# Two more gate tiles as a block-product pair, and a projection summed in two parts

## The chip, the core and the metric

The kernel runs on one core of one Trainium2 chip, as one program with one launch. The metric is the device time of the program in microseconds, the median of several runs. TensorE (PE) does the matmuls, VectorE (DVE) and ScalarE (ACT) the elementwise work, GpSimd (POOL) a little of it, and DMA queues, most of them issued from SyncE (SP), move data between HBM and on-chip memory. Each engine takes its own instructions in the order in which the built program lists them and waits on semaphores for the others.

## The reference

One layer of a two-branch backbone runs on 640 tokens (128 prompt and 512 sample tokens) of width 1024. The part that matters here:

```python
h = x * (1.0 + scale1) + shift1
proj = h @ p['w_in']
q, f_fwd, f_bwd, i_raw, g_raw, hy, mg = jnp.split(proj, SPLIT_IDX, axis=-1)
o_a, s_f, s_b = hgrn2_mixer(q, f_fwd, f_bwd, i_raw, g_raw, lb, ...)     # 8 heads, a scan
o_b = hyena_mixer(hy, p, row_len)                                       # a long convolution
gate_a, gate_b = jnp.split(jax.nn.sigmoid(mg), 2, axis=-1)
mix = (gate_a * (o_a @ p['proj_a']) + gate_b * (o_b @ p['proj_b'])) @ p['w_out']
x = layer_norm(ALPHA * x + gate1 * mix, p['ln1_g'], p['ln1_b'])
```

Inside `hgrn2_mixer` each head's output is divided by its root mean square before `o_a` is projected. A SwiGLU block with a second norm follows. All is float32; the outputs are the tokens of both groups and the final scan states.

## The kernel before

**Tiles and precision.** A dense product for one tile of 128 output channels is done in two halves of 320 tokens. Each float32 operand is split into a rounded high part (a cast, on ACT or DVE) and a low part (a subtraction, mostly on DVE), and three products of the parts are added: 8 slices of the inner dimension times 3 passes are 24 matmuls of 128x320 for a half, 48 for a tile (`dense_fm`). Its weights (512 KB) are loaded into a buffer `raw` by SP and split into `wh` and `wl`, three buffers of each (`issue`, `advance`; `LOOK` says by weight how many are prepared ahead).

**Stages.** The work runs in this order: filters and the modulation vectors; the *product stage* (tiles named m...); the long convolution (hy, fw, inv, then pb, its projection); the *scan stage* of the first branch (f, g, kT, sc, u, o, msp, mga, pa); `w_out` and the first norm (wo); SwiGLU (fa, fb, fc, fo) and the second norm.

**The product stage.** Pairs of tiles of `w_in` are not done densely: with two tiles and two halves of tokens the output is a 2x2 block product, for which class `Wino` needs 7 products of 12 matmuls instead of 8 of them, with sums of weights and of operands ahead and sums of results behind. `M1_ORDER` lists the pairs, and `PLAN` the order of steps: `g13` loads the first weight row of pair 13 and `w13` the second one and makes the sums and splits; `613` is product 6 of pair 13. Products 1, 6, 7, 4 of a pair add up in one bank of PSUM (`ma`): after 6 and after 7 ACT copies the bank (`mu`) before the next product adds to it. Products 5 and 3 share bank `mc`, and product 2 has `mb`. A finished tile goes to a DRAM tensor (`sd`) and is loaded again in its stage (`spilled`). There are 14 pairs; of the gate `mga` (`gate_a`, 8 tiles) tiles 4 to 7 come this way, tiles 0 to 3 are dense in the scan stage.

**The scan stage.** `HGSEQ` lists its steps: `a7 b7 q7 g7` make or load the inputs of head 7, `e7` (`hg_elem`) is its long elementwise chain on DVE and ACT, `s7` (`hg_scan`, `hg_post`) its matmuls: transposes kT of a tile t6, scores sc, states u, outputs o, and the mean square msp. Tiles t4 to t7 have one buffer, so the chain of a head writes them after the scan of the head before has read them. `c` (`comb_open`) opens the memory of the projection and splits heads 0 to 5 (`oah`, `oal`), `m0` to `m7` provide the gate tiles (`gate_unit`), `t` (`hg_tail`) norms and splits heads 6 and 7, `p0` to `p7` (`proja_unit`) project, multiply by the gate and add the other branch's part.

**What sets the order.** A scheduler places each engine's instructions when the program is built, by the order of the steps and its own estimate of when things are ready; an instruction may be placed ahead of others that were written earlier. `order_after` forces one behind another. Matmuls of dense gate tiles are placed where the scan's own matmuls would leave gaps.

## Time and profile before

| | |
|---|---|
| median of 3 runs | 1414.06 us (1412.3 to 1414.61) |
| the profiled execution | 1413.15 us, its span 1411.4 us |
| PE busy | 1371.7 us of the span |
| DVE, ACT, POOL busy | 995.7, 620.0, 63.4 us |
| product stage, from its first ma to the first matmul of the convolution (hy) | 115.5 us to 309.8 us |
| dense gate tiles, start of the first and the last mga matmul | 813.7 us and 858.7 us |

All times below are of this one profiled execution, counted from the start of its span. In a timeline a row gives start, duration, engine, line, operation and tiles (out<-in), and in brackets how long the engine stood idle before it and what it had waited for. Matmuls overlap: each shows some 0.31 us at 128x320, but starts 0.147 us after the one before, so costs are counted from start to start. A row of the waits gives who waited for whom, the total in us, how many times, and the longest.

### The profile page before, as it was taken

What the parts mean: (1) busy time and instruction counts of PE and PEld (TensorE: products, weight loads), DVE (VectorE), ACT (ScalarE), POOL (GpSimd) and SP (SyncE); (2) the same over time, 40 slices, a digit from 0 to 9 for tenths busy, and PEclk for the clock granted to TensorE, in tenths of its full rate; (3) what the DMA queues carried; (4) which work ended last, traced back from release to release, by engine and by line L of the source; (5) the groups of instructions that cost most, each with busy time, mean ns of one, the idle gap of its engine ahead of it and who ended that gap; (6) DMA issues with size and microseconds to landing.
All of it is one profiled execution on the core that took longest, in us unless ns stands there. A gap on an engine that the chain in (4) does not pass through costs nothing. (4 is left out here: it accounts for less than half of the span.)

```text
span 1411.4 us, 23424 instructions
## 1 busy us (share of the span) xinstructions
PE 1371.7 (97%) x9513; PEld 1290.8 (91%) x9513; DVE 995.7 (71%) x1752; ACT 620.0 (44%) x1010; POOL 63.4 (4%) x56
## 2 busy tenths in 40 slices
PE   4999999999999999999999999999999999999997
PEld 2689889899999999999999999988999999998886
DVE  6886786656889743648888786568987776765426
ACT  3555554442323211536655655227654443542121
POOL 4230000010000000000000000000000000000003
PEclk9999999999999999999999999999999999999999
DMA  7944666675323373432222223551653213267211
GB/s 246 334 139 146 208 207 195 184 232 193 101 83 102 90 246 131 135 115 82 81 86 77 64 63 109 174 196 75 169 162 102 81 59 118 89 201 263 75 60 75
DMA packets 198855, 195.63 MB, mean 139 GB/s; under 512 B 7581, under 2 KB 155773, under 8 KB 197980
## 3 DMA queue, kind: packets, MB, share of 16 engines
q1 hardware_dynamic: 194860, 179.75, 40.5%
q0 software_dynamic: 2160, 9.15, 1.8%
q10 hardware_dynamic: 1728, 5.24, 0.9%
q8 instruction: 74, 1.21, 0.4%
q14 instruction: 33, 0.27, 0.1%
HBM read 162.91 MB, written 31.21 MB: 138 GB/s over the span
## 5 line engine op out<-in xcount | busy, mean ns | idle before, releaser
L182 DVE TENSOR_TENSOR wl<-raw,wh 128x1024 fp32r<-128x1024 f32 x96 | 117.3, 1223 | 133.1 <-ACT wh L358 132.3
L358 ACT CAST wh<-raw 128x1024 fp32r<-128x1024 f32 x90 | 94.1, 1049 | 220.9 <-PE pb L612 41.0
L1431 PE MATMUL fo<-wh,act 128*128 128x512 f32 (+1 forms) x440 | 130.7, 380 | 0.0
L1431 PEld LDWEIGHTS fo<-wh,act 128*128 128x128 f32 x440 | 81.2, 188 | 16.0
L1431 PE MATMUL fo<-wl,act 128*128 128x512 f32 (+1 forms) x220 | 83.4, 379 | 0.0
L612 PE MATMUL hy<-hTh,wh 128*128 128x320 f32 x256 | 79.6, 311 | 0.0
L612 PE MATMUL hy<-hTh,wl 128*128 128x320 f32 x256 | 79.1, 309 | 0.0
L612 PE MATMUL hy<-hTl,wh 128*128 128x320 f32 x256 | 79.1, 309 | 0.0
L612 PE MATMUL f<-hTh,wh 128*128 128x320 f32 x224 | 70.7, 316 | 0.0
L612 PE MATMUL f<-hTl,wh 128*128 128x320 f32 x224 | 69.7, 311 | 0.0
L612 PE MATMUL f<-hTh,wl 128*128 128x320 f32 x224 | 69.2, 309 | 0.0
L182 POOL TENSOR_TENSOR y<-y,gb 128x512 f32<-128x512 f32 x8 | 11.6, 1454 | 888.4 <-ACT y L171 888.1
L1431 PEld LDWEIGHTS fo<-wl,act 128*128 128x128 f32 x220 | 41.3, 188 | 7.9
L612 PEld LDWEIGHTS hy<-hTh,wh 128*128 128x128 f32 x256 | 48.1, 188 | 0.0
L612 PEld LDWEIGHTS hy<-hTl,wh 128*128 128x128 f32 x256 | 48.1, 188 | 0.0
L612 PEld LDWEIGHTS hy<-hTh,wl 128*128 128x128 f32 x256 | 48.0, 188 | 0.0
L171 ACT ACT_TABLE_LOAD x36 | 46.2, 1283 | 1.4 <-PEq L1791 0.7
L715 PE MATMUL v<-wl,hTh 128*128 128x256 f32 x160 | 45.0, 286 | 1.6 <-DVE wl L182 1.6
L715 PE MATMUL v<-wh,hTl 128*128 128x256 f32 x160 | 45.1, 284 | 0.1
L715 PE MATMUL v<-wh,hTh 128*128 128x256 f32 x160 | 44.9, 285 | 0.0
L612 PEld LDWEIGHTS f<-hTl,wh 128*128 128x128 f32 x224 | 42.2, 188 | 0.0
L612 PEld LDWEIGHTS f<-hTh,wh 128*128 128x128 f32 x224 | 42.1, 188 | 0.0
(2293 smaller groups left out, 4699.6 us busy)
## 6 DMA issues: line engine op xcount, KB each, us to landing
raw<-in_w_in SPq DMA_DIRECT2D x52, 512.0 KB, 3.8
araw<-in_ada_w SPq DMA_DIRECT2D x20, 1024.0 KB, 6.5
rm<-in_w_in SPq DMA_DIRECT2D x28, 512.0 KB, 4.6
rp<-in_ffn_w_in SPq DMA_DIRECT2D x24, 512.0 KB, 5.4
raw<-in_ffn_w_out SPq DMA_DIRECT2D x22, 512.0 KB, 4.6
rf<-in_ffn_w_in SPq DMA_DIRECT2D x18, 512.0 KB, 5.2
sd<-my SPq DMA_DIRECT2D x28, 320.0 KB, 2.3
kk<-kd SPq DMA_DIRECT2D x20, 256.0 KB, 2.7
```

The source lines that it names most:

```text
L171: r = S.activation(out, in_, func, bias=bias, scale=scale)
L182: return (eng or V).tensor_tensor(out=out, in0=a, in1=b, op=op)
L358: (V.tensor_copy if HIE[i] == "V" else S.copy)(hi, raw)
L612: r = PE.matmul(ps[:, 0:HT], w[a][:, k, :], x[b][:, k, c0:c0 + HT], start=k == 0 and i == 0, stop=k == kt - 1 and i == 2)
L715: PE.matmul(ps[:, (t - t0) * 256:(t - t0) * 256 + 256], hT[b][:, k, t * P:t * P + P], w[a][:, k % 4, :], start=k == 0 and i == 0, stop=k = ...
L1431: PE.matmul(ps, x(t, b, k0 + kk), w[a][:, kk, :], start=first and kk == 0 and i == 0, stop=last and kk == nk - 1 and i == 2)
```

## The change

Gate tiles 2 and 3 of `mga` become pair 14 of the product stage and are then loaded like tiles 4 to 7. Tile 1's matmuls are ordered behind the last o matmul of head 7. Projection tiles 0 and 1 are done in two steps each: `r0 r1` sum over heads 0 to 5 in four banks that stay open, `z0 z1` add heads 6 and 7 and finish. Three entries of `LOOK` (weights 58 to 60) go from 2 to 1.

```diff
 M1_ORDER = (
...
-('mga', 6, 7))
+('mga', 6, 7), ('mga', 2, 3))
...
-                dense_fm(w[0], hT, half, ps)
+                dense_fm(w[0], hT, half, ps, after=hg.get(("end", H - 1)) if j and tag == "mga" else None)
...
-                PE.matmul(o, st[:, 1, 4 - b], q128[:, 1, cs], start=False, stop=True)
+                hg["end", h] = PE.matmul(o, st[:, 1, 4 - b], q128[:, 1, cs], start=False, stop=True)
...
+        elif op == "r":
+            U(proja_first(h), w_fm(I["proj_a"][0], h * P))
+        elif op == "z":
+            U(proja_unit(h))
...
+    def proja_sums(j, k0, k1, w):
+        for half in range(2):
+            cs = slice(half * HT, half * HT + HT)
+            if k0 == 0:
+                cb_[j, half] = mm_bank(f"pa{j}_{half}")
+            ps = cb_[j, half]
+            for k in range(k0, k1):
+                for i, (a, b) in enumerate(PASSES):
+                    PE.matmul(ps[:, 0:HT], w[a][:, k, :], cb_["oa"][b][:, k, cs],
+                              start=k == 0 and i == 0, stop=k == KT - 1 and i == 2)
+
+    def proja_first(j):
+        def fn(w):
+            cb_["w", j] = w
+            proja_sums(j, 0, H - 2, w)
+        return fn
...
-        def fn(w):
+        def fn(*w):
...
+            proja_sums(j, 0 if w else H - 2, KT, w[0] if w else cb_["w", j])
...
-                ps = mm_bank(f"pa{j}_{half}")
-                dense_fm(w, cb_["oa"], half, ps)
+                ps = cb_[j, half]
```

The two lists of steps end like this, before and after:

```
PLAN   ... 712 Q19 513 213 613 412 713 312 413 313 Z9
PLAN   ... 712 Q19 213 g14 613 412 114 w14 312 513 713 413 313 Z9 214 614 514 714 414 314
HGSEQ  ... s6 e7 s7 c m0 m1 t m2 m3 p0 m4 p1 m5 p2 m6 p3 m7 p4 p5 p6 p7
HGSEQ  ... s6 e7 s7 c m0 m1 t r0 r1 m2 z0 m3 z1 m4 p2 m5 p3 m6 p4 m7 p5 p6 p7
```

**Place 1: PE between the scans of heads 6 and 7.** Before, in PE's order from the last mean square of head 6 (msp6) to the scores of head 7 (scp7); mga1_0 is gate tile 1, first half:

```order
L1304 MATMUL msp6_0_8805<-sql6_8802,ones_92 128x384
L612 MATMUL mga0_1_9032<-hTh0_600,wl56_8573 128x320
...
L612 MATMUL mga0_1_9032<-hTh3_888,wl56_8573 128x320
L612 MATMUL mga1_0_9065<-hTh0_600,wh57_8632 128x320
...
L612 MATMUL mga1_1_9091<-hTl2_873,wh57_8632 128x320
L1240 MATMUL kT7_0_8856<-cst_84,t6_7_8819 128x128 x4
L612 MATMUL mga1_1_9091<-hTh2_872,wl57_8633 128x320
...
L612 MATMUL mga2_0_9134<-hTl0_601,wh58_9001 128x320
L1240 MATMUL kT7_1_8863<-cst_84,t6_7_8819 128x128 x4
L1249 MATMUL scp7_8870<-t4_7_8817,t5_7_8818 128x128
```

And with the change:

```order
L1304 MATMUL msp6_0_8937<-sql6_8934,ones_92 128x384
L612 MATMUL mga0_1_9164<-hTh0_600,wl56_8705 128x320
...
L612 MATMUL mga0_1_9164<-hTh3_888,wl56_8705 128x320
L1240 MATMUL kT7_0_8988<-cst_84,t6_7_8951 128x128 x4
L1240 MATMUL kT7_1_8995<-cst_84,t6_7_8951 128x128 x4
L1249 MATMUL scp7_9002<-t4_7_8949,t5_7_8950 128x128
L1249 MATMUL sc7_0_9003<-t4_7_8949,t5_7_8950 128x128 x4
```

Sixty gate matmuls stood ahead of the first transposes kT7_0, 19 of them of tile 0; the 19 are left. The 12 between the two kT are gone too.

**Place 2: PE from the states of head 7 to the projection.** Before (u7 states, o7 outputs, pa0_0 projection tile 0, first half):

```order
L1269 MATMUL u7_1_8930<-vh6_8691,kt7_1_8868 128x128 x4
L612 MATMUL mga2_0_9134<-hTh0_600,wl58_9002 128x320
...
L1280 MATMUL o7_0_8941<-scs7_8917,vh6_8691 128x128 x2
...
L1283 MATMUL o7_0_8941<-t3_7_8816,st7_8854 128x128
L612 MATMUL mga2_0_9134<-hTh2_872,wl58_9002 128x320
...
L612 MATMUL mga3_1_9219<-hTh3_888,wl59_9061 128x320
L612 MATMUL pa0_0_9253<-oah_8985,wh60_9129 128x320
```

With the change:

```order
L1269 MATMUL u7_1_9062<-vh6_8823,kt7_1_9000 128x128 x4
L1280 MATMUL o7_0_9073<-scs7_9049,vh6_8823 128x128 x2
...
L1283 MATMUL o7_0_9073<-t3_7_8948,st7_8986 128x128
L612 MATMUL mga1_0_9197<-hTh0_600,wh57_8764 128x320
...
L612 MATMUL mga1_1_9223<-hTh3_888,wl57_8765 128x320
L1385 MATMUL pa0_0_9259<-oah_9117,wh58_9133 128x320
...
L1385 MATMUL pa1_1_9322<-oah_9117,wl59_9193 128x320
...
L1385 MATMUL pa0_0_9259<-oal_9118,wh58_9133 128x320
...
L1385 MATMUL pa2_0_9399<-oah_9117,wh60_9299 128x320
```

Nine gate matmuls ahead of o7 are gone. Behind it stand the 48 of tile 1 instead of 82. Then come 72 projection matmuls over six heads in four banks (pa0_0, pa0_1, pa1_0, pa1_1), 24 over the last two heads, and tile 2.

**Place 3: PE at the end of the product stage.** Before, from product 7 of pair 13 (its operand is m7) to the first matmul of the convolution stage (hy1_0):

```order
L675 MATMUL ma13_3077<-m7h_1071,wmu13l_3106 128x320
L675 MATMUL mc12_3183<-hTh2_872,wmv12h_2977 128x320
...
L675 MATMUL mc12_3183<-hTh3_888,wmv12l_2978 128x320
L675 MATMUL ma13_3077<-m4h_1073,wma13h_3094 128x320
...
L675 MATMUL mc13_3217<-hTh3_888,wmv13l_3111 128x320
L431 MATMUL adaT9_3346<-cst_84,md9_3344 128x128 x4
L612 MATMUL hy1_0_0_3397<-hTh0_600,wh4_3380 128x320
```

With the change, from product 6 of pair 13 on:

```order
L675 MATMUL ma13_3077<-m6h_1069,wms13l_3102 128x320
L675 MATMUL ma12_2944<-m4h_1073,wma12h_2961 128x320
...
L675 MATMUL ma13_3077<-m7h_1071,wmu13l_3106 128x320
L431 MATMUL adaT9_3389<-cst_84,md9_3387 128x128 x4
L675 MATMUL mb14_3398<-hTh2_872,wmg14h_3235 128x320
L675 MATMUL ma13_3077<-m4h_1073,wma13h_3094 128x320
...
L675 MATMUL ma14_3272<-m7h_1071,wmu14l_3301 128x320
L675 MATMUL ma14_3272<-m4h_1073,wma14h_3289 128x320
...
L675 MATMUL mc14_3428<-hTh3_888,wmv14l_3306 128x320
L612 MATMUL hy1_0_0_3529<-hTh0_600,wh4_3512 128x320
```

Product 4 of pair 12 comes up while pair 14's weights are being made. Product 4 of pair 14 (operand m4) stands right behind product 7 of the same bank; in pair 13 a product of another bank stood between the two, and now the transposes adaT9 and one matmul do. DVE's order from the scan of head 6 up to kT7's input is the same before and after.

## The prediction

> **What bounds the kernel now.** The page comes first.

> ```profile
> span 1411.4 us, 23424 instructions
> PE 1371.7 (97%) x9513; PEld 1290.8 (91%) x9513; DVE 995.7 (71%) x1752; ACT 620.0 (44%) x1010; POOL 63.4 (4%) x56
> PE   4999999999999999999999999999999999999997
> PEclk9999999999999999999999999999999999999999
> ```

> TensorE (PE) is busy in 39 of 40 slices, at full clock: time follows the number of matmuls and the few places where PE waits. The view of waits, PE alone, from 100 to 960 us, names them:

> ```profile
> PE kT L1240 <- DVE t L182: 1.4, 1, 1.4
> PE ma L675 <- ACT mu L684: 0.5, 1, 0.5
> ```

> So there is one wait of size in 860 us: the transposes kT of head 7 wait for VectorE (DVE). The chain of waits gives the rates:

> ```profile
> 848.29 10.71 PE mga L612 x73
> 859.00 56.33 PE pa L612 x384
> 1024.17 1.76 PE fa L675 x12
> ```

> A 320-column matmul costs 0.1467 us in all three forms (10.71/73, 56.33/384, 1.76/12). In the product stage the same form stands as ma, mb, mc.

> **The change, part by part.**

> *Matmuls.* Two dense gate tiles were 2 x 2 halves x 24 = 96 matmuls, now gone from the scan stage: -96 x 0.1467 = -14.08 us. The pair brings 7 products x 12 = 84 into the product stage: +12.32 us. Splitting the projection keeps its 384. Alone this is -1.76 us, 0.12%; about 0.2% is what a measurement of this kernel can tell from no change.

> *What the gate matmuls covered.* PE's timeline around the scan of head 7, before:

> ```profile
> 822.48 0.33 PE L1304 MATMUL msp<-sql,ones 128*128 128x384 f32 x1
> 822.65 0.31 PE L612 MATMUL mga<-hTh,wl 128*128 128x320 f32 x1
> ...
> 831.30 0.31 PE L612 MATMUL mga<-hTl,wh 128*128 128x320 f32 x1
> 832.99 0.63 PE L1240 MATMUL kT<-cst,t 128*128 128x128 f32 x4 [1.39 <-DVE t L182]
> 833.38 0.40 PE L612 MATMUL mga<-hTh,wl 128*128 128x320 f32 x1
> ...
> 835.27 0.63 PE L1240 MATMUL kT<-cst,t 128*128 128x128 f32 x4
> ...
> 839.85 2.05 PE L1269 MATMUL u<-vh,kt 128*128 128x128 f32 x16
> 841.66 0.39 PE L612 MATMUL mga<-hTh,wl 128*128 128x320 f32 x1
> ...
> 843.07 0.60 PE L1280 MATMUL o<-scs,vh 128*128 128x128 f32 x4
> ...
> 845.88 0.39 PE L612 MATMUL mga<-hTh,wl 128*128 128x320 f32 x1
> ```

> From 822.65 to 831.30 stand 60 gate matmuls: 19 end tile 0, 41 are of tile 1. Twelve more stand between the two kT, nine ahead of o. After the change only the 19 are left ahead of kT: tile 1 is ordered behind the last o of head 7, tiles 2 and 3 are gone. DVE's order up to kT is the same as before, and it is what kT waits for:

> ```profile
> 832.03 0.82 DVE L182 TENSOR_TENSOR t<-t,gg 128x640 f32<-128x640 f32 x1
> ...
> 834.30 0.82 DVE L182 TENSOR_TENSOR t<-t,ff 128x640 f32<-128x640 f32 x1
> ...
> 835.77 1.22 DVE L182 TENSOR_TENSOR wl<-raw,wh 128x1024 fp32r<-128x1024 f32 x1
> ...
> 841.43 0.83 DVE L182 TENSOR_TENSOR scs<-scz 128x640 f32<-128x640 f32 x1
> ...
> 849.46 3.77 DVE L182 TENSOR_TENSOR oal<-oa,oah 128x640 fp32r<-128x640 f32 x5 [1.67 <-ACT oah L1319]
> ```

> The first kT needs the row at 832.03 (ends 832.85; PE starts 0.14 later). PE now arrives at 822.65 + 19 x 0.1467 = 825.44 and still starts at 832.99: a wait of 7.55 us, where from the end of the last gate matmul (831.30 + 0.147) it was 1.54. The second kT needs the row at 834.30 (ends 835.12): it starts near 835.26 as before, with 1.8 us empty. The o matmuls need scs (ends 842.26) and start near 842.40, where nine gate matmuls held PE to 843.07: 0.67 earlier. All waits there: 7.55 + 1.8 + 0.74 = 10.1 us, against 1.6. Behind the waiting kT stands PE's whole queue, and its matmuls are what DVE and ACT wait for next, so nothing makes it up.

> *After the scan.* Before, 82 gate matmuls and the msp ones separate o from the projection (845.88 to 859.00, where the chain's row of pa begins); now 48 do. The projection starts at 859.00 - 0.67 - 34 x 0.1467 = 853.34. It needs the split heads: ACT's and DVE's splits of heads 0 to 5 (the row at 849.46 is five of them, 0.754 each) would run from 848.8 to 853.3, while head 5 is first read at 853.34 + 15 x 0.1467 = 855.5. So 72 matmuls over six heads last to 863.90. Meanwhile the norm of heads 6 and 7:

> ```profile
> 853.43 0.83 ACT L171 ACTIVATE ms<-ms,eps_rms 128x640 f32<-128x640 f32 x1
> 854.27 1.28 ACT L171 ACT_TABLE_LOAD   x1
> 855.57 1.37 ACT L171 ACTIVATE ms<-ms 128x640 f32<-128x640 f32 x2
> ```

> ACT now does a weight cast (1.05 by the cast of the same shape below, from 853.3, when tile 1's matmuls free its buffer), a sigmoid (0.44) and a table load first, then both Ln (1.5), a load, both Exp: Exp ends near 860.2, the last split near 862.7. It is needed at 863.90 + 3 x 0.1467 = 864.3. I cost it at nothing; with that cover of 1.6 us gone, each further us of delay adds itself. The rest is 384 matmuls as before, so the stage ends 859.00 - 853.34 = **5.66 us** earlier. It lost 14.08 us of matmuls: 8.4 us of the gain is eaten by the waits.

> *End of the product stage.* Pair 14's second weight row is issued on SP's queue behind a store of a pair 11 output, and ACT's casts of it stand ahead of a copy (mu, of pair 12's bank) that PE needs. Nearest rows:

> ```profile
> 282.99 0.69 DVE L182 TENSOR_TENSOR wma13l<-rm,wma13h 128x512 fp32r<-128x512 f32 x1 [3.71 <-ACT wma13h L620]
> 285.65 1.05 ACT L620 CAST wmu13h<-rm 128x1024 fp32r<-128x1024 f32 x1 [1.83 <-DVE rm L182]
> 286.86 0.43 ACT L684 COPY mu<-ma 128x320 f32<-128x320 f32 x1 [0.16 <-PE ma L675]
> ...
> 294.39 0.42 ACT L684 COPY mu<-ma 128x320 f32<-128x320 f32 x1 [1.15 <-PE ma L675]
> 295.23 0.41 PE L675 MATMUL mc<-m5h,wmu13h 128*128 128x320 f32 x1
> rm<-in_w_in SPq DMA_DIRECT2D x28, 512.0 KB, 4.6
> ```

> The sigmoid whose store goes ahead now stands just before the first of these copies, so I estimate the weights' issue at 287.7 and, with the median of 4.6 us, their landing at 292.3. Two casts (0.62 for the half, 1.05) with two sums on DVE between (0.69 each, one split) let the second copy end near 296.8; PE's product 4 of pair 12 wants it at 295.23 + 24 x 0.1467 = 298.75. No wait, though with a landing 2 to 3 us later there is one. Product 4 of pair 14 follows product 7 with nothing between, and product 4 of pair 13 nearly so: each waits for the copy of its bank, the 0.5 us of the second row of waits above. I take 0.9 for both, 0 and 2.5 as ends. Other edits: one pair's DVE and ACT work beside 12 us of products (DVE stood idle for 3.71 us ahead of pair 13's), two stores and two loads of 320 KB, all under PE; price 0.

> *The clock.* PE has not waited 7.5 us in this kernel since its first stage. What shorter gaps do:

> ```profile
> 79.04 0.43 PE L586 MATMUL k<-abh,kth 128*128 128x256 f32 x1 [2.08 <-DVE af L182]
> 75.90:79.20 3.30, 1.22 (x10) 1.01 (x10) 0.91 (x2) 1.48 (x4) 2.36 (x2) 1.00 0.89 280
> 79.30:82.60 3.30, 3.30 (x17) 3.30 (x17) 3.30 (x6) 3.09 (x6) 1.89 (x1) 0.50 0.34 97
> 82.70:86.00 3.30, 3.30 (x29) 3.30 (x29) 3.30 (x6) 3.14 (x5) 1.58 (x1) 1.00 0.39 155
> ```

> These are windows of busy time by engine (first number: PE's). In 3.3 us with PE busy for 1.22, the granted clock (PEclk) stayed 1.00; in the next 3.3 us it was 0.50, and PE did 17 matmuls where it then did 29. Such a window, all busy, costs about 3.4 x (1 - 17/29) = 1.4 us (3.4: a little over the 3.3 asked for). A 7.55 us wait holds at least one empty window, so PE comes back at half clock. The first kT lies in the shadow of the second; from 835.3 the clock is half for what is left of one window, sometimes two. Ends 0 and 2.8; I take 1.2. [...]

> **Sum**: +12.32 - 5.66 + 0.9 + 1.2 = **+8.8 us**. The profiled execution took 1413.15 us, so 1421.9; that one lies 0.9 under the median of the runs (1414.06), which would give 1422.8. I say **1422.3**, slower by 0.6%.

> **Rivals.**

> *DVE keeps up, the waits go (not slower).* If head 7's chain on DVE were ready when PE arrives at 825.4, only the 12 matmuls count: 1413.15 - 1.76 = 1411.4. It decides below about 2 us of new waits. For it: the same transposes of head 6 show no wait in the view above. Against: the chain could give back only the weight split that stands in it (1.22 us, as the row at 835.77) of the 6 us needed, and it stands there still.

> *The clock stays low through the scan.* Its matmuls are small and wait again (1.8, 0.74 us). If every window from 833 to 845 were half, 9.2 us of PE work becomes 9.2 x 29/17 = 15.7: +6.5 instead of 1.2, 1427.6. Against: the window after 82.70 above was full again after a single one.

> *A second wait in the product stage*: pair 14's weights land 3 us later: 1422.3 + 2.2 = 1424.5.

> *The split does not cover the norm*: the last splits come 2 us late: 1422.3 + 0.6 = 1422.9; inside the range.

> **How the numbers follow.** Forecast with its small terms anywhere between their ends: 0.80 (the late weights and the late norm are in it). Clock low through the scan: 0.05. About half of the head 7 wait gone (1416 to 1418): 0.07. DVE keeps up: 0.08. Lowest of the forecast: 1412.3, the fastest run, + 6.66 = 1419, less one weight split (1.22): 1417.8. Highest: 1414.06 + 6.66 + 2.5 + 2.8 = 1426. Range 1418 to 1426.5. Slower by over 0.2% (above 1416.9): 0.90; within: 0.07; faster (under 1411.2): 0.03.

> **What would show it.** In the profile after: the wait of PE kT for DVE t at 7 to 8 us instead of 1.4, a second one near 1.8 for the second kT, and one under 1 us at o; PEclk under 1.00 in the few us behind; the scan of head 7 some 12 to 14 us later than before, the end of the projection (before 859.00 + 56.33 = 915.33) 7 to 9 us later. No wait at the two heads added last to the projection, or one under 1 us. Wrong would be: PE passing the first kT of head 7 without a wait over 4 us, or a wait over 3 us anywhere else between 290 and 330 us.

## The result and the profile after

The changed kernel took 1422.47 us, the median of four runs (1420.53 to 1426.12); the kernel before took 1413.29 (four runs, 1412.3 to 1414.61). The ratio is 1.0071, with a 95% interval of 1.0056 to 1.0086: slower by 0.7%, where 1422.3 was forecast. The profiled execution took 1420.53 us.

First the page: the span, the busy times, and the two rows of 40 slices for PE and for its granted clock.

```profile
span 1418.6 us, 23429 instructions
PE 1371.2 (97%) x9501; PEld 1290.1 (91%) x9501; DVE 1002.7 (71%) x1762; ACT 621.4 (44%) x1015; POOL 63.4 (4%) x56
PE   4999999999999999999999979999999999999997
PEclk9999999999999999999999989999999999999999
```

PE has 12 matmuls fewer. Slice 24 (815.7 to 851.2 us) fell from 9 to 7: a hole near 840 us. The clock row has an 8 in the same slice. The view of waits of PE from 100 to 960 us (who waited for whom, total, times, longest) names the hole:

```profile
PE kT L1240 <- DVE t L182: 8.6, 2, 7.4
PE ma L675 <- ACT mu L684: 1.3, 2, 0.7
PE v L715 <- DVE wl L182: 0.7, 1, 0.7
PE o L1280 <- DVE scs L182: 0.5, 1, 0.5
```

The wait of the transposes kT was 1.4 in all, and is 8.6; the wait at o is new (the one of v, 0.7, was there before). In PE's timeline, and then in the chain of waits:

```profile
836.32 0.31 PE L612 MATMUL mga<-hTh,wl 128*128 128x320 f32 x1
844.02 1.09 PE L1240 MATMUL kT<-cst,t 128*128 128x128 f32 x4 [7.40 <-DVE t L182]
846.30 1.09 PE L1240 MATMUL kT<-cst,t 128*128 128x128 f32 x4 [1.19 <-DVE t L182]
...
856.07 0.68 PE L1280 MATMUL o<-scs,vh 128*128 128x128 f32 x4 [0.49 <-DVE scs L182]
```

```profile
861.38 5.71 PE mga L612 x39
867.09 56.32 PE pa L1385 x384
923.41 38.42 PE wo L1452 x168
```

The same four transposes that took 0.63 us took 1.09: PE came back at half clock. With these rows and those shown of before, the span splits so (first ma and first hy are the ends of the product stage; kT is the first one of head 7):

| stage, us | before | after | difference | forecast |
|---|---|---|---|---|
| start to first ma | 115.52 | 113.94 | -1.58 | 0 |
| first ma to first hy | 194.25 | 206.99 | +12.74 | +13.22 |
| first hy to kT | 523.22 | 523.09 | -0.13 | 0 |
| kT to projection (pa) | 26.01 | 23.07 | -2.94 | -4.46 |
| projection | 56.33 | 56.32 | -0.01 | 0 |
| its end to the end of the span | 496.07 | 495.19 | -0.88 | 0 |
| span | 1411.4 | 1418.6 | +7.2 | +8.8 |

The first and last rows are not the change's work: PE lists the same matmuls there. In the first one the granted clock differs: it was 0.50 for two stretches of 3.41 us before and, from 23 us on, for none after. The large terms fell where they were forecast, with one error of 1.5 us, in the stretch behind kT.

### The profile page after: what moved, and what is told of

The parts are those of the page before. It is cut to its first block, busy times and chain, and to the rows that moved or that the text cites. A ratio compares the mean times of both kernels' runs of the same rounds, so it can differ in the third digit from the quotient of the medians.

```text
span 1418.6 us, 23429 instructions
## 1 busy us (share of the span) xinstructions
PE 1371.2 (97%) x9501; PEld 1290.1 (91%) x9501; DVE 1002.7 (71%) x1762; ACT 621.4 (44%) x1015; POOL 63.4 (4%) x56
## 4 chain that ended last, share of the span: by engine, by line
PE 52%; DVE 4%; ACT 1%; DMA 1%; SPq 0%; issue 0%; DVEq 0%
PE fo L1452 10%; PE fa L675 9%; PE f L612 7%; PE fc L675 5%; PE pa L1385 4%; PE g L612 3%; PE wo L1452 3%; PE fb L675 2%; PE sc L1249 1%; PE u L1269 1%; PE v L715 1%; PE mga L612 1%; PE o L1280 1%; PE fo_last L1452 1%; DMA rp<-in_ffn_w_in 1%; PE kT L1240 1%
## 5 line engine op out<-in xcount | busy, mean ns | idle before, releaser
L182 DVE TENSOR_TENSOR wl<-raw,wh 128x1024 fp32r<-128x1024 f32 x94 | 114.8, 1223 | 133.4 <-ACT wh L358 132.7
L612 PE MATMUL hy<-hTh,wh 128*128 128x320 f32 x256 | 79.5, 311 | 0.0
L612 PE MATMUL hy<-hTh,wl 128*128 128x320 f32 x256 | 79.1, 309 | 0.0
L612 PE MATMUL hy<-hTl,wh 128*128 128x320 f32 x256 | 79.1, 309 | 0.0
L612 PE MATMUL f<-hTh,wh 128*128 128x320 f32 x224 | 70.7, 316 | 0.0
L612 PE MATMUL f<-hTl,wh 128*128 128x320 f32 x224 | 69.6, 311 | 0.0
L612 PE MATMUL f<-hTh,wl 128*128 128x320 f32 x224 | 69.2, 309 | 0.0
L182 POOL TENSOR_TENSOR y<-y,gb 128x512 f32<-128x512 f32 x8 | 11.6, 1453 | 885.2 <-ACT y L171 884.8
L612 PEld LDWEIGHTS hy<-hTh,wh 128*128 128x128 f32 x256 | 48.1, 188 | 0.0
L612 PEld LDWEIGHTS hy<-hTl,wh 128*128 128x128 f32 x256 | 48.1, 188 | 0.0
L612 PEld LDWEIGHTS hy<-hTh,wl 128*128 128x128 f32 x256 | 48.1, 188 | 0.0
L612 PEld LDWEIGHTS f<-hTl,wh 128*128 128x128 f32 x224 | 42.2, 188 | 0.0
L612 PEld LDWEIGHTS f<-hTh,wh 128*128 128x128 f32 x224 | 42.1, 188 | 0.0
## 6 DMA issues: line engine op xcount, KB each, us to landing
raw<-in_w_in SPq DMA_DIRECT2D x50, 512.0 KB, 3.8
rm<-in_w_in SPq DMA_DIRECT2D x30, 512.0 KB, 4.6
rp<-in_ffn_w_in SPq DMA_DIRECT2D x24, 512.0 KB, 5.1
raw<-in_ffn_w_out SPq DMA_DIRECT2D x22, 512.0 KB, 3.9
rf<-in_ffn_w_in SPq DMA_DIRECT2D x18, 512.0 KB, 4.3
```

The lines of the kernel that those rows point to most:

```text
L182: return (eng or V).tensor_tensor(out=out, in0=a, in1=b, op=op)
L612: r = PE.matmul(ps[:, 0:HT], w[a][:, k, :], x[b][:, k, c0:c0 + HT], start=k == 0 and i == 0, stop=k == kt - 1 and i == 2)
```

## The experiments

Each kernel was timed beside the kernel before on the same chip (medians 1414.10, 1413.25 and 1413.21 in the three groups). The columns: median and ratio with its interval; then, from the profile, first ma to first hy, first hy to the first matmul of w_out (wo), PE's longest wait at kT of head 7, and how long the granted clock was 0.50 in the scan of head 7 or just behind.

| kernel | us | ratio | ma to hy | hy to wo | kT wait | half clock |
|---|---|---|---|---|---|---|
| before | 1413.3 | 1 | 194.3 | 605.4 | 1.4 | 0 |
| changed | 1422.47 | 1.0071 (1.0056 to 1.0086) | 207.0 | 602.3 | 7.4 | 10.2 |
| e1 tile 1 not ordered | 1416.81 | 1.0018 (1.0009 to 1.0027) | 209.4 | 597.0 | 1.4 | 3.4 |
| e2 half of it ordered | 1418.99 | 1.0039 (1.0027 to 1.0052) | 207.9 | 599.2 | 3.9 | 6.8 |
| e3 wait filled | 1421.19 | 1.0053 (1.0040 to 1.0066) | 208.6 | 599.6 | 1.4 | 0 |
| e5 projection whole | 1426.00 | 1.0091 (1.0077 to 1.0104) | 210.1 | 603.3 | 7.4 | 10.2 |
| e6 end of PLAN | 1425.75 | 1.0077 (1.0063 to 1.0091) | 211.5 | 602.1 | 7.4 | 10.2 |
| e7 g shifted, before | 1416.65 | 1.0022 (1.0013 to 1.0031) | 194.6 | 608.0 | 1.4 | 0 |
| e8 g shifted, changed | 1418.06 | 1.0034 (1.0020 to 1.0047) | 206.9 | 595.6 | 1.4 | 0 |
| e9 e8 and e2 | 1416.70 | 1.0019 (1.0010 to 1.0028) | 206.9 | 594.5 | 1.4 | 0 |
| e10 chain to POOL | 1424.89 | 1.0080 (1.0068 to 1.0092) | 207.1 | 603.7 | 9.8 | 13.7 |
| e12 next weights to POOL | 1424.39 | 1.0078 (1.0066 to 1.0090) | 209.0 | 601.9 | 7.4 | 10.2 |
| e13 both, before | 1418.38 | 1.0032 (1.0021 to 1.0043) | 193.7 | 609.6 | 4.4 | 3.4 |
| e14 both on e9 | 1420.72 | 1.0053 (1.0041 to 1.0065) | 210.4 | 598.6 | 4.4 | 6.8 |

### Where the scan stage gives its gain back

The theory: the forced order of tile 1 takes away the work that covered DVE's chain, and the wait brings the clock down. **e1** drops the order:

```diff
-dense_fm(w[0], hT, half, ps, after=hg.get(("end", H - 1)) if j and tag == "mga" else None)
+dense_fm(w[0], hT, half, ps)
```

> The changed kernel with tile 1's matmuls no longer ordered behind the last o of head 7; the scheduler puts 41 of them ahead of the first kT of head 7, 7 between the two, none behind the scan. Theory (the cover lost at kT is the main cost, the clock the second): the wait at the first kT falls from 7.5 us to 1.4, at the second from 1.5 to 0.8, no half-clock window there; in return the projection stands right behind the scan and waits for the splits of heads 0 to 5 and for the norm of heads 6 and 7, 2 to 5 us in all. Time 1416 to 1419, 4 to 6 us under the changed kernel. Rival (forcing the order costs nothing, the loss is in the product stage): 1421 to 1424.

As expected: 1416.81 us, the wait at kT back to 1.4, no half clock in the scan. The price is behind the scan, in PE's timeline:

```profile
860.53 0.39 PE L1283 MATMUL o<-t,st 128*128 128x128 f32 x2
862.04 0.56 PE L1303 MATMUL msp<-sqh,ones 128*128 128x384 f32 x2 [1.12 <-ACT sqh L1300]
862.44 0.64 PE L1304 MATMUL msp<-sql,ones 128*128 128x256 f32 x2
864.27 1.21 PE L1385 MATMUL pa<-oah,wh 128*128 128x320 f32 x4 [1.19 <-ACT oah L1319]
```

The projection waits for its first split. Ordering tile 1 behind the scan bought its cover there at a loss: hy to wo is 5.3 us shorter without it (597.0 against 602.3).

**e2** orders only the second half (`if j and half and tag == "mga"`).

> Only the second half of tile 1 is ordered behind the last o of head 7: 24 matmuls (3.5 us) stand ahead of the first kT, 24 behind the scan. Theory: the wait at the first kT falls from 7.5 us to about 4.0, at the second kT and at o it stays 1.5 and 0.65; the projection waits about 1 us for its splits. Where a wait of 4 us still brings the clock down, 1419.5 to 1421; where it doesn't, 1417 to 1419. Rival (the loss is elsewhere): 1421 to 1424.

Measured 1418.99, wait at kT 3.9. The clock did fall, for two windows, though the time lies in the range given for a clock that stays; of the 1 us expected ahead of the projection 0.67 came, in pieces too small for a row of the waits (first pa to wo took 56.99 us, 56.32 in the changed kernel). From kT to o it is 11.76 us, where e3 below has 9.40 at full clock. Both were errors of the expectation, in opposite directions.

**e3** leaves every needed instruction in place and fills the wait with work, the 48 matmuls of tile 1 done once more in advance:

```diff
                 ps = mm_bank(f"{tag}{j}_{half}")
+                if j == 1 and tag == "mga" and half == 0:
+                    for x in range(2):
+                        dense_fm(w[0], hT, x, ps)
```

> The changed kernel with tile 1's 48 matmuls done twice: the first time into the same bank, unordered, with a result that is overwritten, so that 41 of them stand in the wait at the first kT and 7 in that at the second. Nothing that is needed moves; the waits turn into work, and PE doesn't stand idle. Theory (the clock falls to half after the wait and costs some 2.6 us until it opens): no half-clock window behind 840 us, kT to o 10.1 to 10.7 us instead of 12.05, time 2 to 3 us under the changed kernel, 1419.5 to 1420.5. Rival (the longer scan is DVE's and the time from kT to o does not hang on the clock): time as the changed kernel, 1422 to 1423, kT to o still 12.

PE's timeline of e3, with kT at the same distance from the first gate matmul as in the changed kernel (19.26 us):

```profile
845.87 0.63 PE L1243 MATMUL kT<-cst,t 128*128 128x128 f32 x4 [1.39 <-DVE t L182]
...
848.15 0.63 PE L1243 MATMUL kT<-cst,t 128*128 128x128 f32 x4 [0.62 <-DVE t L182]
...
855.27 0.68 PE L1283 MATMUL o<-scs,vh 128*128 128x128 f32 x4 [0.49 <-DVE scs L182]
```

From kT to o it is 9.40 us, 12.05 in the changed kernel: **2.65 us are the clock's**. The windows of busy time (PE's is the first number of a row, its clock the one behind the five engines) show why it was more than forecast. The changed kernel, then e3 in its three windows from just before the first kT:

```profile
838.37:841.78 3.41, 0.00 (x0) 0.00 (x0) 3.41 (x4) 3.39 (x7) 0.00 (x0) 1.00 0.00 0
841.78:845.19 3.41, 1.09 (x4) 0.72 (x4) 3.41 (x6) 1.52 (x4) 0.00 (x0) 0.50 0.52 154
845.19:848.61 3.42, 2.31 (x11) 2.34 (x12) 2.50 (x5) 1.13 (x2) 0.00 (x0) 0.50 0.02 5
848.61:852.02 3.41, 3.41 (x35) 3.19 (x36) 0.00 (x0) 0.00 (x0) 0.00 (x0) 0.50 0.00 0
852.02:855.43 3.41, 3.41 (x68) 3.26 (x64) 2.20 (x6) 0.00 (x0) 0.00 (x0) 1.00 0.00 0
```

```profile
842.22:845.63 3.41, 2.26 (x16) 2.00 (x14) 3.41 (x4) 2.88 (x6) 0.00 (x0) 1.00 0.44 133
845.63:849.05 3.42, 2.56 (x19) 2.35 (x20) 3.42 (x7) 0.82 (x2) 0.00 (x0) 1.00 0.07 21
849.05:852.46 3.41, 3.41 (x75) 3.25 (x74) 0.52 (x3) 0.35 (x1) 0.00 (x0) 1.00 0.02 5
```

In the changed kernel one window is empty; the next two hold waits and don't open the clock; only the third, full one does. 35 matmuls stand in it where 68 fit at full clock. The time of e3, 1421.19, is above what was expected; its difference from the changed kernel, 1.3 us, is not told apart by the intervals, so the 2.65 rest on the two timelines. In these rows a window filled to two thirds changed nothing in either direction (2.31 of 3.42 us at half clock, 2.26 of 3.41 in e3 at full clock). The fall came here after an empty window (0.00 us); in e6 below it came after one with PE busy for 1.13 us.

### What the split of the projection is worth

**e5** keeps all but the split: `... s7 c m0 m1 t p0 m2 p1 m3 m4 p2 ...`.

> The changed kernel with projection tiles 0 and 1 done whole, as before the change (p0, p1), the rest left as it is; the scheduler then puts 44 matmuls of heads 0 to 5 ahead of the first one of head 6, instead of 72. Theory (the split in two parts hides the norm of heads 6 and 7): head 6 is wanted 28 x 0.1467 = 4.1 us earlier, its split had 1.9 us of cover in the changed kernel, so PE waits 2 to 2.5 us in the projection, time 2 to 2.5 us over the changed kernel, 1423 to 1426. Rival (nothing is gained by the two parts): no wait at pa, time as the changed kernel.

The view of waits has the row that was expected, somewhat smaller:

```profile
PE pa L1385 <- ACT oah L1319: 1.4, 1, 1.4
```

From the first pa to wo it took 57.97 us, 56.32 in the changed kernel: the split is worth 1.65 us. So two tiles summed over six heads do hide the norm of heads 6 and 7. The times (1426.0 against 1422.47) hold more than that, since in e5's profile the product stage (by 3.1 us) and the stretch ahead of it (by 3.3) were longer too.

### What spreads the times

Two of the four runs of the changed kernel lie near 1420.7, two at 1424.1 and 1426.1. **e6** swaps the last two steps of PLAN (`714 314 414` for `714 414 314`).

> The last steps of the product stage stand as 714 314 414 instead of 714 414 314: product 3 of pair 14 (12 matmuls, 1.76 us) stands between product 7 and product 4, whose bank ACT copies meanwhile. Theory: the wait of 0.67 us of PE ma for ACT mu at the end of the product stage goes, time 0.5 to 0.8 us under the changed kernel, within what can't be told apart by the time alone; the row in the view of waits tells. Rival: product 3's bank is waited for in its place and nothing changes.

Both ideas missed: the scheduler left the first four matmuls of product 4 in their place and moved only the eight behind them, so the wait of 0.67 us stayed. As PE's order is otherwise that of the changed kernel, e6 is nearly a repeat, and its five runs spread alike (1421.78 to 1427.07). Its profile is of the longest one. PE's timeline at product 4 of pair 13, the windows there, and DVE's rows ahead:

```profile
310.78 0.42 PE L675 MATMUL ma<-m4h,wma13h 128*128 128x320 f32 x1 [2.28 <-ACT mu L684]
```

```profile
308.00:311.41 3.41, 1.13 (x9) 0.91 (x8) 2.39 (x6) 1.23 (x2) 0.00 (x0) 1.00 0.78 253
311.41:314.82 3.41, 3.41 (x15) 3.41 (x14) 2.65 (x14) 0.91 (x2) 0.00 (x0) 0.50 0.24 96
314.82:318.20 3.38, 3.38 (x25) 3.38 (x24) 0.94 (x2) 1.07 (x2) 0.00 (x0) 1.00 0.31 122
```

```profile
294.03 0.69 DVE L182 TENSOR_TENSOR wma14l<-rm,wma14h 128x512 fp32r<-128x512 f32 x1 [1.98 <-ACT wma14h L620]
...
297.40 0.69 DVE L358 CAST wh<-raw 128x1024 fp32r<-128x1024 f32 x1 [1.22 <-DMA raw<-in_w_in]
298.01 0.68 DVE L182 TENSOR_TENSOR rm<-rm,rm 128x512 f32<-128x512 f32 x1
```

A cast for the convolution's first weight stands in DVE's queue among pair 14's sums; here its load was late, DVE stood for 1.22 us, and everything behind it with it. PE lost 2.5 us at product 4 and, at half clock behind it, some 1.4 more (15 matmuls where the next window has 25: 3.41 x 10/25). In the profile of the changed kernel that cast began without a wait and neither happened. First ma to first hy took 211.5 us against 207.0: this one place makes 3.9 of these 4.5 us (the spans differ by 6.6, of which 1.7 lie ahead of the first ma). With DVE's order there unchanged, five of nine profiles with the pair show no wait over 0.25 us there, the others 0.35, 0.91, 1.98 and 2.52.

**e12** takes the two casts and the split of the next stage's weights off DVE (cast and subtraction of weights 4 and 5 on `G`, which is POOL).

> The changed kernel with the casts and splits of the first two weights of the convolution (two casts of 0.69 us, one split of 1.22) moved from DVE to POOL: on DVE they stood among the sums of pair 14's weights, the first one behind a load. PE's order is unchanged. Theory (pair 14's sums wait in DVE's queue behind a weight of the next stage whose load is late in some executions; PE then waits at product 4 of pair 13 for ACT's copy and its clock falls): no wait at product 4 of pair 13 in any profile, no half-clock window near 311 us, the stage from the first ma to the first hy 206.5 to 207.5 us, and the times lie together at 1420 to 1422.5 with none above 1424. Rival (the spread of the times comes from the first stage or from the load of pair 14's own weights): times spread from 1420.5 to 1427 as in the two runs of this order so far.

It failed: the wait at product 4 is 2.29 us in its profile, the times 1422.83 to 1425.63. DVE's timeline, then POOL's:

```profile
293.88 2.17 DVE L182 TENSOR_TENSOR rm<-rm,rm 128x512 f32<-128x512 f32 x2
296.07 2.78 DVE L182 TENSOR_TENSOR rm<-rm 128x512 f32<-128x512 f32 x1
```

```profile
295.58 2.73 POOL L182 TENSOR_TENSOR wl<-raw,wh 128x1024 fp32r<-128x1024 f32 x1
```

A sum that takes 0.69 us elsewhere took 2.78 and ended 0.54 us behind POOL's subtraction. So e12 replaced one blockage by another, and whether the queue order alone makes the spread stays open: the late cast is seen in e6 alone. In e1 and e5, with waits of 0.91 and 1.98 at product 4, this first cast did not wait for its load; the second one did, for 1.26 and 1.38 us where the changed kernel has 0.66. The same collision was already in the changed kernel, in a DVE row that took 0.88 us before the change:

```profile
300.18 2.64 DVE L808 SCALAR_TENSOR_TENSOR my<-mx,prT,my 128x630 f32<-128x630 f32 x1 [0.29 <-ACT my L171]
```

POOL worked on its own split from 299.42 to 302.15 there. In all nine profiles counted above this row took 2.60 to 3.01 us, 2.67 in e6, and it lies in the chain that product 4 of pair 13 waits for: DVE's sum mx stands behind it, an activation of ACT waits for mx, and the copy of the bank stands behind that. ACT's timeline in e6:

```profile
309.49 0.92 ACT L171 ACTIVATE my<-mx,prT 128x640 f32<-128x640 f32 x1 [4.00 <-DVE mx L182]
310.32 0.40 ACT L684 COPY mu<-ma 128x320 f32<-128x320 f32 x1
```

So the late cast alone does not make e6's wait. Without the 1.79 us that the row took above 0.88, some 0.7 of the 2.52 would be left, an estimate. A kernel that only moves POOL's split to another engine was not tried.

The rival of e12's expectation holds in part as well: the stretch from the start to the first ma, where pair 14 has no part, takes 113.9 to 117.6 us in the fourteen profiles. It goes with the clock: 113.9 and 114.6 with no half-clock window from 23 us on (changed kernel, e8), 117.2 and 117.6 with four (e5, e7).

### Can the pair be made to pay?

**e10** shortens the chain that kT waits for. The chain of waits of the changed kernel has two foreign pieces in it:

```profile
839.87 1.14 DVE wl L182
841.00 1.40 DVE t L182
842.41 0.73 DVE oa L182
843.14 3.02 DVE t L182 x5
```

They go to POOL (weight 59's subtraction, head 5's norm product).

> The changed kernel with two operations that stand in DVE's chain of head 7 without belonging to it moved to POOL: the weight split wl of projection tile 1 (1.13 us from start to start) and the norm product of head 5 (0.74). PE's order is unchanged; on DVE one product (0.73) now stands ahead of the one that the first kT needs. Theory (the wait at kT is DVE's in-order chain): the wait at the first kT falls from 7.5 to 6.4 us, from 1.5 to about 0.8 at the second, 1.9 us in all; the clock is still half for about 10 us; time 1.9 us under the changed kernel. Rival (something else releases kT, or POOL slows DVE): waits unchanged, or DVE's rows in the chain longer than 1.48 and 0.82 us.

The rival won. DVE's timeline and POOL's:

```profile
841.23 1.48 DVE L182 TENSOR_TENSOR t<-t,sg 128x1280 f32<-128x1280 f32 x1
843.09 3.18 DVE L182 TENSOR_TENSOR t<-t,sg 128x1280 f32<-128x1280 f32 x1 [0.37 <-ACT t L171]
846.19 2.15 DVE L182 TENSOR_TENSOR t<-t,ff 128x640 f32<-128x640 f32 x1
```

```profile
842.02 2.90 POOL L182 TENSOR_TENSOR wl<-raw,wh 128x1024 fp32r<-128x1024 f32 x1 [323.68 <-ACT wh L358]
844.89 2.76 POOL L182 TENSOR_TENSOR oa<-oa,ms 128x640 f32<-128x640 f32 x1
```

1.87 us left DVE, but a product of 0.73 came ahead of the one that kT needs, as expected, and two products grew by 1.70 and 1.33 us while POOL worked, with a further 0.37 of waiting: 2.3 us more in sum, and kT came 2.4 us later, not earlier. That kT follows DVE's chain is thereby shown the other way round: longer chain, longer wait (9.8 us), one more window at half clock.

**e7, e8, e9** find cover elsewhere: the tile g of a head is made behind the scan of the head before (`s6 e7 g7 s7` for `g7 s6 e7 s7`, for all heads), so 48 more matmuls lie in the chain of head 7. e7 is this on the kernel before, e8 on the changed one, e9 with e2's half order.

> The kernel before, with the tile g of each head made behind the scan of the head before it instead of ahead (a7 b7 q7 s6 e7 g7 s7): the same work and the same matmuls between two scans, but 48 more that can stand in the chain of head 7. Theory (the wait at kT is DVE's chain against the cover that is at hand): 65 matmuls ahead of the first kT instead of 60, so its wait falls from 1.5 to about 0.8 us, time 1412 to 1414. Rival (g's sigmoid and products now stand in the chain of head 7 and lengthen it): wait at kT 2 to 4 us, 1415 to 1418.

> The changed kernel with the tile g of each head made behind the scan of the head before it (as in the run with before). 65 matmuls then stand ahead of the first kT of head 7 again, although tile 1 is still ordered behind the last o. Theory: wait at the first kT 0.8 to 1.5 us instead of 7.5, no half clock, the waits at the second kT (0.8) and at o (0.65) stay; 8 to 9.5 us under the changed kernel, 1413 to 1415. Rival (the chain of head 7 is what lasts, whatever covers it): 1420 to 1423.

> As the run before, with only the second half of tile 1 ordered behind the last o: the first half's 24 matmuls fill the second kT (5), the o (9) and the stretch behind. Theory: waits at kT and o together under 1.5 us, none or under 1 us ahead of the projection, no half clock: 1411.5 to 1414, 0 to 2 us under the kernel before (1.76 us fewer matmuls, 0.9 us of waits at the end of the product stage). Rival (the projection comes too early and waits for its splits): a wait at pa of 2 us or more, 1414 to 1416.

The waits came out as expected (kT 1.4, no half clock; e9 has no wait at the second kT or at o), the times did not: 1416.65, 1418.06 and 1416.70. The shift costs 2.6 us of its own on the kernel before (hy to wo 608.0 against 605.4): 0.4 us at the v tiles, about 0.27 us in each head from the third on, and 0.8 us ahead of wo. e9 shortens hy to wo by 10.9 us; with the shift's 2.6 added that is 13.5 of the 14.08 us of matmuls that left, an estimate over two profiles. So with its cover restored the scan stage gives nearly all of the matmuls' time back, and what is left is the pair's +12.7 in the product stage against it.

**e13** and **e14** put both moves to POOL on the kernel before and on e9 (in e14 weight 58's subtraction too).

> The kernel before with both moves to POOL: the two weights of the convolution, and the weight split and norm product in head 7's chain. The scheduler then sets the first kT of head 7 four gate matmuls earlier. Theory: the wait at kT falls from 1.5 to about 1.0 us or less, the small waits at the end of the product stage (0.5 of ma for mu) go; time 0.5 to 1.5 us under the kernel before, hardly to be told apart. [...]

> The changed kernel with the best of the runs so far: g made behind the scan, only half of tile 1 ordered behind the last o, and on POOL the weights of the convolution, two weight splits and a norm product out of head 7's chain. Theory: product stage 206.5 to 207.5 us, wait at the first kT under 1 us, none at the second or at o; 1.5 to 3 us under the run with g shifted and half of tile 1 (1416.7), so 1413.5 to 1415.5: about the kernel before, not under it, since g behind the scan has cost 2.5 us of its own. Rival: no better than that run, 1416 to 1417.5.

Both are slower than what they started from, by 5 and 4 us, with a wait at kT of 4.4 us: they have e10's moves in them, and e14 a wait of 3.0 us at product 4 of pair 13 as well. No version run here beats the kernel before.

## Why the prediction was right, and where it was off

- **Matmuls, +12.32 and -14.08.** Right: 9513 matmuls became 9501, and first ma to first hy grew by 12.74, where 13.22 was forecast with the waits.
- **The waits in the scan.** Forecast 7.55, 1.8 and 0.74 us from DVE's rows and PE's new arrival. Counted from start to start, less the usual distance of such rows, they are 7.56, 1.50 and 0.65. The second was shorter because the first kT ran at half clock and so ended later. e1 and e2 move the wait with the number of matmuls ahead (1.4, 3.9, 7.4 us for 41, 24 and none of tile 1) while kT itself stays at the same place behind hy (523.1 us in all): it is DVE that sets it.
- **After the scan.** Nothing waits ahead of the projection and none at the two heads added last. The last split ended at 876.49 (874.93 and 1.56 for two), and head 7 was wanted at 878.09 (867.09 and 75 matmuls): the cover of 1.6 us, as forecast. e5 shows that without the split 1.65 us would be lost.
- **The clock was the mis-sized term.** "From 835.3 the clock is half for what is left of one window, sometimes two", 1.2 us, failed. It was the author's estimate, and no run shows it: the clock was half for three windows and cost 2.65 (e3), inside the ends of 0 and 2.8. The step took a window to open the clock that was partly idle; the second wait stood in it, and with PE busy for 2.31 of 3.42 us the clock stayed at half. The size differed between executions: in e5, e6 and e12, with the same waits and order up to o and the same 10.2 us of half clock, kT to o took 11.26, 11.80 and 11.67 us, so the clock cost 1.9 to 2.4 there. In the prediction's own rows the fall came without an empty window: PE was busy for 1.22 of the 3.3 us ahead of it. The excess over 1.2 is the 1.5 us by which kT to projection misses (-2.94 against -4.46).
- **End of the product stage, 0.9.** Product 4 of pair 14 waits 0.67, more than its half of the 0.9. For product 4 of pair 13 the price is nil in the profile of the changed kernel and about 3.9 us in the longest of the others: the rival of the late weights, priced 2.2, is real in part of the executions, and costs more than its price because the clock falls there too. Its step blamed the landing of pair 14's row; in e6 the queue of DVE added more to it than the row itself, which was late by 0.9 us against the copies around it, and the collision with POOL, which the prediction does not have, another 1.8.
- **The sum.** +8.8 was forecast, +9.2 is the difference of the medians, +7.4 that of the two profiled executions. Agreement to half a microsecond is partly luck: the clock came out 1.5 us dearer, the first and last stretches of the profiled execution were 2.5 us shorter, and the spread of the product stage fills the rest.
- **Slips in the working that change nothing.** PE shows a 9 in 38 of the 40 slices, not in 39. The wait of 0.5 of ma for mu, which gave 0.9 its size, stands at pair 2 (155.2 us), not at the end of the product stage; e13's expectation has it there too. Last splits 2 us late would have cost 0.4 (2 less the cover of 1.6), not 0.6.

Of the rivals, DVE did not keep up, and the clock did not stay low through the whole scan, though it came nearer to that than its chance of 0.05 says.

## What to carry to other kernels

Before matmuls are taken out of a stage, look at what they stand in front of: 14 us of dense work here was also the cover of one in-order DVE chain and of one norm, and 11 of the 14 us (hy to wo fell by 3.1) went into the waits it had filled and the clock behind them. Count such a wait with the clock behind it: with the 7.4 us at kT came 10.2 us of half clock, which cost 2.65. And an engine that is idle was no free relief for a busy one here (in e10 1.87 us left DVE, and its chain became 2.3 us longer): try what the two do to each other first.

## What the runs showed of the hardware that was not expected

```profile
305.39:308.81 3.42, 2.06 (x16) 1.83 (x14) 3.38 (x5) 0.20 (x1) 1.55 (x1) 1.00 0.43 119
308.81:312.22 3.41, 1.73 (x11) 1.73 (x12) 2.39 (x6) 1.23 (x2) 0.00 (x0) 1.00 0.57 194
```
